# A hybrid HGRN2 and DeltaNet layer: HGRN's first decays made earlier, early tiles in DRAM, state steps in the DeltaNet's buffers

## The chip, the core and the metric

The kernel runs on one core of a Trainium2 chip. The metric is the device time of one execution in microseconds. The engines are PE (TensorE, the matrix engine), ACT (ScalarE), DVE (VectorE), POOL (GpSimd) and SP (SyncE, which here issues loads). Each has its own queue of instructions; DMAs are issued from the queues of SP and POOL.

## The reference

One decoder layer for 512 positions of width 1024. Two token mixers read the same normalised input and are merged by gates; a SwiGLU feed-forward follows.

```python
proj = jnp.einsum('btd,de->bte', rms_norm(x, pre_mix_w), w_in)
# HGRN2: f = lb + (1-lb) sigmoid(f_logit), k = 1 - f,
# S_t = diag(f_t) S_{t-1} + k_t i_t^T, o_t = S_t^T q_t; in chunks:
bc = jnp.cumsum(log_f)                                  # within a chunk
decay = jnp.exp(where(causal, b_c[i] - b_c[j], -inf))   # per channel d
attn = jnp.einsum('bhid,bhjd,bhijd->bhij', q_c, k_c, decay)
o = attn @ v_c + (q_c * jnp.exp(b_c)) @ S
S = S * jnp.exp(b_last) + (k_c * jnp.exp(b_last - b_c)).T @ v_c
# gated DeltaNet: S_t = alpha_t (I - beta_t k_t k_t^T) S_{t-1} + beta_t k_t v_t^T
# chunked with T = (I + A)^-1, A strictly lower triangular
merged = sigmoid(m_a) * (o_a @ w_o_hg) + sigmoid(m_b) * (o_b @ w_o_dn)
h = x + rms_norm(merged @ w_out, post_mix_w)
return h + rms_norm((silu(gate) * up) @ w_down, post_ffn_w)
```

HGRN's decay is per channel, so `attn` is not one matmul of q and k.

## The kernel before

All products are made in three matmuls of split numbers: each float32 operand is a high part (a cast on ACT, L108 for weights, L120 for data) and a low part (a subtraction on DVE, L109 or L146), and `mm3` adds high by high, high by low and low by high. `dense_in` takes one weight tile of 128 output features (512 KB, loaded by SP into `raw`), splits it into `whi` and `wlo`, and runs 24 matmuls of 128x512 into one of three banks `mm`; an evacuation function then empties the bank. The names hg_q, hg_f, hg_g, dn_q, dn_v, dn_g, m_a and m_b are four (or eight) such weight tiles each; hg_q[1] is the second tile of hg_q.

The sequence of work that bears on the change: hg_f, dn_q, dn_v and dn_g are projected. `l2` normalises the DeltaNet's key and query; its column sums (`colsum`, L376 and L377) are matmuls with ones, one for the high and one for the low half of the squares, placed behind named dense matmuls. `dn_sub` runs a forward substitution on POOL in 62 instructions, writes its result to the DRAM scratch `scr` (L460, L462) and reads it back (L483, L486). `hg_prep` makes k (`hk`) and the cumulative log decay b (`hf`) from the f logits, in four chunks of 128 positions. hg_q and half of hg_g are then projected and kept in six `hct` buffers, while `dn_inv` (L479 to L523) completes the DeltaNet's inverse with small matmuls placed between the dense ones; `dn_prep` and `dn_step` run the DeltaNet over its chunks. After it the slots of the DeltaNet's key and query take HGRN's q (`hq`) and gate (`ghg`), into which POOL copies the six buffers (L792, L794). The gate m_b0 is written to DRAM as `early_b` (L786) and read back at L809.

`hg_attn(c)` builds the attention of one chunk from pieces of halving block size, lev = 64, 32, 16, 8, 4, 2. For each lev it makes a tile E of decays, from half of b minus a reference column (two subtractions on POOL, L146), an exponential on ACT (L660), and multiplications by q and by k on DVE (L146); four matmuls of E by itself follow (L667 for lev 64 and 32, L673 below), and their result is copied under a mask into the attention AT (L669, L674). `hg_step(c)` carries the state. Chunk c+1's attention is interleaved with chunk c's step and with dense matmuls of m_b0, hg_g, the DeltaNet's output projection `y_proj` and m_b1.

Buffers are pools: `dct` of nine and `hct` of seven tiles of 128x512, banks `dps` (three) and `hps` (two). Which instruction stands where in a queue is decided by the scheduler of the tile framework at build time, by priorities and estimated times; on the chip each queue runs in that order. POOL's queue holds its subtractions and the DMAs that it issues.

## Time and profile before

| | us |
|---|---|
| median of 3 runs (lowest to highest) | 858.56 (858.18 to 858.79) |
| profiled execution | 856.74 |
| its span in the trace | 855.0 |
| PE busy | 821.0 (96%) |
| DVE busy | 585.6 (68%) |
| ACT busy | 485.4 (57%) |
| POOL busy | 136.9 (16%) |

The profiled execution's own time is 1.74 us above its span, and 1.82 us below the median of the runs. The mean granted clock of TensorE in it was 0.988. Busy shares are averages over the whole program; what ends a wait at one place is read from the timeline there. In the rows further down a time is the microseconds from the span's start. A bracket at the end of a row is the idle time of that engine just before, with what ended it. The duration of an ACT or DVE row includes about 0.1 us in which the next one is already under way, so spacings of starts are a little smaller.

### The profile page before, as it was taken

Reading aid. Unit: us, or ns where it says so; the run is one execution under the profiler, and the core shown is the slowest. Engines: PE = TensorE matmul, PEld = TensorE weight load, DVE = VectorE, ACT = ScalarE, POOL = GpSimd, SP = SyncE. Lnnn points to the kernel's source line nnn. Section 1 sums busy time; section 2 is a strip of 40 time slices with the busy share of each in tenths; the row PEclk is TensorE's granted clock in tenths of the full one; section 3 lists DMA queues with packets and bytes.
Section 4 is the critical chain, followed back from the end, with each engine's and each line's share of the span. In section 5 each row is a group of like instructions: output and inputs, shape, how many; then the busy total and the mean of one; then the engine's idle time right before and its main releaser. Section 6 shows DMA issues by size and latency. Waiting matters only on the chain.

```text
span 855.0 us, 12316 instructions
## 1 busy us (share of the span) xinstructions
PE 821.0 (96%) x4677; PEld 689.3 (81%) x4677; DVE 585.6 (68%) x903; ACT 485.4 (57%) x884; POOL 136.9 (16%) x187
## 2 busy tenths in 40 slices
PE   9998999999997999899999999999999998999995
PEld 8886887767876877788888898999999997876774
DVE  4794998625557788862664797787787787557545
ACT  6658798945376466585443365545455456445443
POOL 1420178300034245430010300000000000000000
PEclk9998999999999999999999999999999999999999
DMA  8425532712126112253211313322413404556552
GB/s 294 153 94 177 140 108 74 179 51 74 38 86 209 51 49 87 87 173 97 86 53 49 123 50 100 116 82 99 145 54 99 148 24 141 181 172 206 186 175 99
DMA packets 34907, 98.53 MB, mean 115 GB/s; under 512 B 4192, under 2 KB 4608, under 8 KB 34720
## 3 DMA queue, kind: packets, MB, share of 16 engines
q1 hardware_dynamic: 32112, 88.65, 31.5%
q0 software_dynamic: 2736, 9.09, 4.0%
q8 instruction: 37, 0.61, 0.3%
q14 instruction: 22, 0.18, 0.1%
HBM read 91.95 MB, written 5.78 MB: 114 GB/s over the span
## 4 chain that ended last, share of the span: by engine, by line
PE 66%; DVE 12%; DMA 11%; ACT 6%; issue 3%; POOL 0%; SPq 0%; DVEq 0%; ACTq 0%; POOLq 0%
PE mm L116 20%; PE mm L117 11%; DMA raw<-in_w_down_dram 8%; DVE wlo L109 3%; PE hps L116 3%; ACT whi L108 3%; DVE hct L146 3%; PE hps L1041 2%; PE hps L1040 2%; PE hps L1042 2%; PE hps L117 2%; DVE s L149 2%; PE hps L673 2%; DVE s L146 1%; PE mm L898 1%
## 5 line engine op out<-in xcount | busy, mean ns | idle before, releaser
L116 PE MATMUL mm<-s,whi 128*128 128x512 f32 (+1 forms) x992 | 310.5, 392 | 0.0
L109 DVE TENSOR_TENSOR wlo<-raw,whi 128x1024 fp32r<-128x1024 f32 x108 | 135.5, 1254 | 116.2 <-ACT whi L108 111.7
L116 PEld LDWEIGHTS mm<-s,whi 128*128 128x128 f32 x992 | 184.3, 190 | 36.5 <-issue 0.2
L117 PE MATMUL mm<-s,wlo 128*128 128x512 f32 (+1 forms) x496 | 196.9, 397 | 0.2 <-DVE wlo L109 0.2
L108 ACT CAST whi<-raw 128x1024 fp32r<-128x1024 f32 x108 | 113.1, 1047 | 80.2 <-DMA raw<-in_w_down_dram 37.9
L117 PEld LDWEIGHTS mm<-s,wlo 128*128 128x128 f32 x496 | 94.0, 189 | 20.2 <-DVE wlo L109 0.7
L146 POOL TENSOR_TENSOR s<-s,dct 128x512 f32<-128x512 f32 (+1 forms) x9 | 12.7, 1437 | 391.0 <-DVE s L149 362.1
L120 ACT CAST whi<-raw 128x512 fp32r<-128x512 f32 (+1 forms) x64 | 38.9, 617 | 28.2 <-PE mm L1041 10.1
L120 ACT CAST whi<-s 128x512 fp32r<-128x512 f32 x42 | 25.9, 617 | 49.4 <-PE mm L116 23.6
L1040 PE MATMUL hps<-s,whi 128*128 128x256 f32 x168 | 47.2, 281 | 0.4 <-DVE hct L146 0.4
L1041 PE MATMUL hps<-s,whi 128*128 128x256 f32 x168 | 47.2, 281 | 0.1
L1042 PE MATMUL hps<-s,wlo 128*128 128x256 f32 x168 | 46.9, 279 | 0.0
L146 DVE TENSOR_TENSOR wlo<-raw,whi 128x512 fp32r<-128x512 f32 (+1 forms) x64 | 43.5, 688 | 2.4 <-ACT whi L120 1.6
L146 POOL TENSOR_TENSOR hct<-s 128x256 f32<-128x256 f32 (+1 forms) x55 | 38.2, 724 | 25.8 <-DVE hct L146 8.6
L116 PE MATMUL hps<-s,whi 128*128 128x512 f32 (+1 forms) x144 | 40.8, 368 | 0.0
L146 DVE TENSOR_TENSOR hct<-hct,s 128x256 f32<-128x256 f32 (+1 forms) x63 | 35.0, 601 | 4.6 <-ACT hct L624 2.0
L146 POOL TENSOR_TENSOR s<-s 128x126 f32<-128x126 f32 (+22 forms) x62 | 34.8, 561 | 10.5 <-DMA s<-scr 5.7
L1040 PEld LDWEIGHTS hps<-s,whi 128*128 128x128 f32 x168 | 31.5, 188 | 0.9 <-DVE hct L146 0.6
L1041 PEld LDWEIGHTS hps<-s,whi 128*128 128x128 f32 x168 | 31.7, 188 | 0.6 <-DVE s L146 0.3
L1042 PEld LDWEIGHTS hps<-s,wlo 128*128 128x128 f32 x168 | 31.7, 189 | 0.0
L1041 PE MATMUL mm<-s,whi 128*128 128x256 f32 x112 | 31.5, 281 | 0.0
L1040 PE MATMUL mm<-s,whi 128*128 128x256 f32 x112 | 31.4, 281 | 0.0
(325 smaller groups left out, 1850.0 us busy)
## 6 DMA issues: line engine op xcount, KB each, us to landing
raw<-in_w_in_a_dram SPq DMA_DIRECT2D x44, 512.0 KB, 3.4
raw<-in_w_down_dram SPq DMA_DIRECT2D x44, 512.0 KB, 3.4
s<-in_w_gu_dram SPq DMA_DIRECT2D x56, 256.0 KB, 4.1
raw<-in_w_gu_dram SPq DMA_DIRECT2D x16, 512.0 KB, 3.6
raw<-in_w_o_dram SPq DMA_DIRECT2D x8, 512.0 KB, 3.5
dct<-in_w_out_dram SPq DMA_DIRECT2D x16, 256.0 KB, 4.2
raw<-in_w_iab_dram SPq DMA_DIRECT2D x8, 260.0 KB, 5.9
s<-in_xT_dram SPq DMA_DIRECT2D x8, 256.0 KB, 6.0
```

The costliest lines, as they stand in the source:

```text
L108: nc.scalar.copy(hi[:, :n], raw[:, :n])
L109: nc.vector.tensor_tensor(out=lo[:, :n], in0=raw[:, :n], in1=hi[:, :n].bitcast(F32), op=ALU.subtract)
L116: return [mm(ps, lh, rh, start=start, stop=False), mm(ps, lh, rl, start=False, stop=False), mm(ps, ll, rh, start=False, stop=stop)]
L117: mm(ps, ll, rh, start=False, stop=stop)]
L120: self.nc.scalar.copy(hi, src)
L146: (eng or self.nc.vector).tensor_tensor(out=out, in0=a, in1=b, op=op)
L149: self.nc.vector.scalar_tensor_tensor(out=out, in0=a, scalar=s, in1=b, op0=op0, op1=op1)
L673: T.matmul(ps[:, h, :], E[:, h, :], E[:, h, :], start=True, stop=True)
L898: T.matmul(ps, mh, wl, start=False, stop=False)
L1040: mm(ps, wh[:, k, :], ah[k], start=start and k == 0, stop=False, skip_group_check=True)
L1041: mm(ps, wh[:, k, :], al[k], start=False, stop=False, skip_group_check=True)
L1042: mm(ps, wl[:, k, :], ah[k], start=False, stop=k == 3, skip_group_check=True)
```

## The change

The two subtractions, the exponential and the multiplication by k of a decay tile move into a function `hg_decay`. For chunk 0 and lev 64, 32, 16, 8 and 4 it is called right behind the call of `dn_inv`, and the five tiles stay in `hct` until HGRN's first chunk uses them; the multiplication by q remains in `hg_attn`. The early tiles of hg_q, hg_g and m_b0 pass through one buffer `out` and are written to DRAM; q and the first half of the gate are read back by five DMAs instead of six POOL copies. HGRN's column sums, its lev 1 tile, its state steps and its head norm use `dct` buffers, and the state steps and the head norm use `dps` banks. The query's l2 column sums move from dn_v to dn_g, and `gates_late` is placed behind the key's norm. For hg_g, `gge` is changed like `qe` below.

```diff
+    def spill(self):
+        return self.tp.tile([P, 512], F32, tag="out", name=self.name("out"), bufs=1)
...
     def l2(self, y, qscale, after):
...
-            if qscale:
-                A.activation(t, t, AF.Exp, scale=-0.5, bias=self.lnqs)
-            else:
+            e = A.activation(t, t, AF.Exp, scale=-0.5, bias=self.lnqs) if qscale else \
                 A.activation(t, t, AF.Exp, scale=-0.5)
-            self.tt(y[:, h, :], y[:, h, :], t, ALU.mult)
+            m = nc.vector.tensor_tensor(out=y[:, h, :], in0=y[:, h, :], in1=t, op=ALU.mult)
+        return e, m
...
-    def hg_attn(self, c, out):
+    def hg_decay(self, c, lev):
+        v = lambda x: x.rearrange("p h (n two t) -> p (h n) two t", two=2, t=lev)
+        n = NH * P // (2 * lev)
+        E = self.hct()
+        Ev, bv, kv = v(E), v(self.hf[:, c]), v(self.hk[:, c])
+        ref = bv[:, :, 0, lev - 1:lev].to_broadcast([P, n, lev])
+        self.tt(Ev[:, :, 1, :], bv[:, :, 1, :], ref, ALU.subtract, self.nc.gpsimd)
+        self.tt(Ev[:, :, 0, :], ref, bv[:, :, 0, :], ALU.subtract, self.nc.gpsimd)
+        self.nc.scalar.activation(E, E, AF.Exp)
+        self.tt(Ev[:, :, 0, :], Ev[:, :, 0, :], kv[:, :, 0, :], ALU.mult)
+        return E
+
+    def hg_attn(self, c, out, decays={}):
...
-        pr = self.hct()
+        pr = self.dct()
...
-        ps = self.colsum(pr.rearrange("p h t -> p (h t)"), self.hct, self.hps)
+        ps = self.colsum(pr.rearrange("p h t -> p (h t)"), self.dct, self.hps)
...
-            E = self.hct()
-            Ev, bv, qv, kv = v(E), v(b), v(q), v(k)
-            ref = bv[:, :, 0, lev - 1:lev].to_broadcast([P, n, lev])
-            self.tt(Ev[:, :, 1, :], bv[:, :, 1, :], ref, ALU.subtract, nc.gpsimd)
-            self.tt(Ev[:, :, 0, :], ref, bv[:, :, 0, :], ALU.subtract, nc.gpsimd)
-            A.activation(E, E, AF.Exp)
+            E = decays[lev] if lev in decays else self.hg_decay(c, lev)
+            Ev, qv = v(E), v(q)
             self.tt(Ev[:, :, 1, :], Ev[:, :, 1, :], qv[:, :, 1, :], ALU.mult)
-            self.tt(Ev[:, :, 0, :], Ev[:, :, 0, :], kv[:, :, 0, :], ALU.mult)
...
     def hg_step(self, c, AT):
...
-        o = self.hps()
+        o = self.dps()
...
-            kd = self.hct()
+            kd = self.dct()
...
-            ps = self.hps()
+            ps = self.dps()
...
-            kt = self.hct()
+            kt = self.dct()
...
-        return self.head_norm(c, o, self.ghg, self.ohg, self.hct, self.hps)
+        return self.head_norm(c, o, self.ghg, self.ohg, self.dct, self.dps)
...
     def mixers(self):
...
-        self.l2(self.kT, False, [self.log["hg_f"][i] for i in (30, 34, 38, 42)])
+        norm = self.l2(self.kT, False, [self.log["hg_f"][i] for i in (30, 34, 38, 42)])
...
-        self.gates_late()
+        with self.tc.issue_after(norm[0].ins), self.tc.issue_after(norm[1].ins):
+            self.gates_late()
...
-        self.l2(self.qT, True, [self.log["dn_v"][i] for i in (38, 50, 62, 74)])
...
+        self.l2(self.qT, True, [self.log["dn_g"][i] for i in (6, 18, 30, 42)])
-        early, eg = {}, {}
+        early_q, early_g, early_b = (self.dp.tile([n, P, S], F32, name=f"early_{t}") for n, t in ((4, "q"), (2, "g"), (4, "b")))
         def qe(i, ps):
-            early[i] = self.hct((P, 512))
-            A.copy(early[i], ps)
+            t = self.spill()
+            A.copy(t, ps)
+            nc.gpsimd.dma_start(out=early_q[i], in_=t)
...
         self.dn_inv((self.log["hg_q"] + self.log["hg_g"])[43::3])
+        early_e = {lev: self.hg_decay(0, lev) for lev in HG_LEVELS[:5]}
...
         def gate_out(ft, ps):
-            t = self.hct((P, 512))
+            t = self.spill()
...
-        for i in range(4):
-            nc.gpsimd.tensor_copy(self.hq[:, :, i, :], early[i].rearrange("p (c t) -> p c t", c=NC_))
-        for i in range(2):
-            nc.gpsimd.tensor_copy(self.ghg[:, i, :], eg[i])
+        for c in range(NC_):
+            nc.gpsimd.dma_start(out=self.hq[:, c], in_=early_q[:, :, c * P:c * P + P].rearrange("f p t -> p f t"))
+        nc.gpsimd.dma_start(out=self.ghg[:, :2], in_=early_g.rearrange("f p t -> p f t"))
...
-        run(self.hg_attn(0, at))
+        run(self.hg_attn(0, at, early_e))
```

Line numbers of the changed kernel are three or four higher up to `hg_prep` (L108 is L112 there, L146 is L150), and up to twelve higher behind it (L667 is L677, L786 is L798).

**POOL, from the end of the DeltaNet's forward substitution.** `scr` is its scratch, `early_b` the m_b0 gate. Before:

```order
L460 DMA scr_649<-s_119_787 64x32x16 x2
L462 DMA scr_650<-s_119_787 64x16x32 x2
L483 DMA s_253_1793<-scr_649 32x16x32 x2
L486 DMA s_118_786<-scr_650 128x8x128 x2
L786 DMA early_b<-hct_2271 128x512
L786 DMA early_b<-hct_2307 128x512
```

The changed kernel, where `hct_1979` to `hct_1999` are the five decay tiles of chunk 0 and `s_92` is b:

```order
L463 DMA scr_649<-s_119_787 64x32x16 x2
L465 DMA scr_650<-s_119_787 64x16x32 x2
L486 DMA s_253_1802<-scr_649 32x16x32 x2
L489 DMA s_118_786<-scr_650 128x8x128 x2
L150 TENSOR_TENSOR hct_1979<-s_92_672 128x4x64 x2
L150 TENSOR_TENSOR hct_1984<-s_92_672 128x8x32 x2
L150 TENSOR_TENSOR hct_1989<-s_92_672 128x16x16 x2
L150 TENSOR_TENSOR hct_1994<-s_92_672 128x32x8 x2
L150 TENSOR_TENSOR hct_1999<-s_92_672 128x64x4 x2
L769 DMA early_q<-out_1623 128x512
```

The ten subtractions stand between the reads of the scratch and the first write of an early tile.

**ACT, around the weight cast for hg_q[1].** `s_210` is k and `s_92` b, `s_193` is the gate of dn_g, whose third tile is `mm_1400`, and `whi_1623` the weights of hg_q[1]. Before:

```order
L108 CAST whi_1623<-raw_1622 128x1024
L141 ACTIVATE s_193_1323<-mm_1400 128x512
L618 ACTIVATE s_210_1464<-s_210_1464,sm_638 128x128
L142 ACTIVATE s_193_1323<-s_193_1323,one 128x512
L620 ACTIVATE hct_1549<-s_92_672,sm_639 128x128
L143 ACTIVATE s_193_1323<-s_193_1323 128x512
L618 ACTIVATE s_210_1464<-s_210_1464,sm_638 128x128
```

The changed kernel, with dn_g's gate as `s_177`, its third tile as `mm_1352` and the weights of hg_q[1] as `whi_1627`:

```order
L623 ACTIVATE hct_1552<-s_92_672,sm_639 128x128
L642 ACTIVATE hct_1979<-hct_1979 128x512
L112 CAST whi_1627<-raw_1626 128x1024
L145 ACTIVATE s_177_1275<-mm_1352 128x512
L626 ACTIVATE hct_1552<-hct_1552 128x512
L146 ACTIVATE s_177_1275<-s_177_1275,one 128x512
L627 ACTIVATE hct_1552<-hct_1552,one 128x512
L147 ACTIVATE s_177_1275<-s_177_1275 128x512
L642 ACTIVATE hct_1984<-hct_1984 128x512
L642 ACTIVATE hct_1989<-hct_1989 128x512
L642 ACTIVATE hct_1994<-hct_1994 128x512
L642 ACTIVATE hct_1999<-hct_1999 128x512
```

The exponential of the first decay tile stands ahead of the cast and of the evacuation of dn_g's third tile, and the other four stand behind that evacuation.

**DVE, at the third step of the DeltaNet.** `s_299` is the DeltaNet's output, `wlo_2530` the low weights of the second late tile of hg_g, and `dct_2216` the low half of a column sum. Before:

```order
L146 TENSOR_TENSOR dct_2173<-dct_2115,dct_2172 128x512
L146 TENSOR_TENSOR dct_2117<-dct_2117,dct_2115 128x512
L146 TENSOR_TENSOR s_299_2047<-dct_2117,s_298_2046 128x4x128
L109 TENSOR_TENSOR wlo_2530<-raw_2528,whi_2529 128x1024
L146 TENSOR_TENSOR dct_2213<-dps_2202,s_193_1323 128x512
L146 TENSOR_TENSOR dct_2216<-dct_2168,dct_2215 128x512
L146 TENSOR_TENSOR dct_2228<-dct_2211,dct_2227 128x512
```

The changed kernel, with the output as `s_304`, the low weights as `wlo_2537`, the low half as `dct_2250`, and HGRN's q as `s_371`:

```order
L150 TENSOR_TENSOR dct_2207<-dct_2149,dct_2206 128x512
L150 TENSOR_TENSOR dct_2151<-dct_2151,dct_2149 128x512
L150 TENSOR_TENSOR hct_1979<-hct_1979,s_371_2417 128x4x64
L150 TENSOR_TENSOR hct_1984<-hct_1984,s_371_2417 128x8x32
L150 TENSOR_TENSOR s_304_2081<-dct_2151,s_303_2080 128x4x128
L150 TENSOR_TENSOR hct_1989<-hct_1989,s_371_2417 128x16x16
L150 TENSOR_TENSOR hct_1994<-hct_1994,s_371_2417 128x32x8
L150 TENSOR_TENSOR hct_1999<-hct_1999,s_371_2417 128x64x4
L113 TENSOR_TENSOR wlo_2537<-raw_2535,whi_2536 128x1024
L150 TENSOR_TENSOR dct_2247<-dps_2236,s_177_1275 128x512
L150 TENSOR_TENSOR dct_2250<-dct_2202,dct_2249 128x512
```

The five multiplications of the decay tiles by q stand ahead of the weight split and of the DeltaNet's column sum.

**PE, at the first L667 of HGRN** (L677 in the changed kernel). `mm_2534` is the second late tile of hg_g and `mm_3040` the first of the DeltaNet's output projection. Before:

```order
L116 MATMUL mm_2534<-s_64_568,whi_2529 128x512
L116 MATMUL mm_2534<-s_66_570,whi_2529 128x512
L117 MATMUL mm_2534<-s_64_568,wlo_2530 128x512
L667 MATMUL hps_2422<-hct_2416 64x64 x4
L667 MATMUL hps_2434<-hct_2428 32x32 x4
L116 MATMUL mm_3040<-s_298_2046,whi_3035 128x512
L116 MATMUL mm_3040<-s_299_2047,whi_3035 128x512
L117 MATMUL mm_3040<-s_298_2046,wlo_3036 128x512
```

The changed kernel, where `mm_2506` is the first late tile of hg_g and `hps_2444` the column sum of lev 1:

```order
L380 MATMUL hps_2444<-dct_2440,onesr 128x256
L677 MATMUL hps_2449<-hct_1979 64x64 x3
L381 MATMUL hps_2444<-dct_2441,onesr 128x256
L677 MATMUL hps_2449<-hct_1979 64x64
L120 MATMUL mm_2506<-s_64_568,whi_2501 128x512
L120 MATMUL mm_2506<-s_66_570,whi_2501 128x512
L121 MATMUL mm_2506<-s_64_568,wlo_2502 128x512
L677 MATMUL hps_2456<-hct_1984 32x32 x4
L683 MATMUL hps_2468<-hct_1989 128x128 x4
```

The first decay matmuls come 28 instructions earlier, within the tile ahead.

## Rows read from the trace of the kernel before

**Rows 1.** The page: busy time, share of the span and instructions of each engine.

```profile
PE 821.0 (96%) x4677; PEld 689.3 (81%) x4677; DVE 585.6 (68%) x903; ACT 485.4 (57%) x884; POOL 136.9 (16%) x187
```

**Rows 2.** Stretches: length, busy of PE, PEld, DVE, ACT, POOL, clock, DMA share, GB/s.

```profile
258.60:370.30 111.70, 101.23 (x594) 81.09 (x593) 90.96 (x144) 65.93 (x118) 48.81 (x67) 0.97 0.28 90
275.40:281.60 6.20, 6.13 (x37) 5.24 (x37) 4.56 (x6) 1.66 (x4) 1.91 (x2) 0.51 0.22 67
300.00:320.00 20.00, 18.17 (x107) 14.03 (x105) 17.33 (x30) 12.63 (x22) 9.87 (x13) 1.00 0.13 46
320.00:340.00 20.00, 19.53 (x123) 15.71 (x119) 18.04 (x31) 13.02 (x24) 9.04 (x12) 1.00 0.25 80
340.00:360.00 20.00, 16.65 (x108) 13.66 (x109) 15.55 (x24) 13.28 (x24) 11.43 (x16) 1.00 0.27 83
```

**Rows 3.** Timeline of PE: start, duration, instruction, and idle time before it.

```profile
141.36 0.50 PE L377 MATMUL dps<-dct,onesr 128*128 128x512 f32 x1 [1.51 <-DVE dct L146]
...
177.70 0.43 PE L479 MATMUL dps<-s,dct 32*32 32x32 f32 x8
...
256.15 0.50 PE L377 MATMUL dps<-dct,onesr 128*128 128x512 f32 x1 [1.05 <-DVE dct L146]
...
269.90 0.63 PE L116 MATMUL mm<-s,whi 128*128 128x512 f32 x2
270.37 0.40 PE L117 MATMUL mm<-s,wlo 128*128 128x512 f32 x1
275.47 1.69 PE L667 MATMUL hps<-hct 128*64 128x64 f32 x16 [4.71 <-DVE hct L146]
...
344.10 0.65 PE L667 MATMUL hps<-hct 128*64 128x64 f32 x8 [1.98 <-DVE hct L146]
```

**Rows 4.** Timeline of POOL, where the change takes away or adds work.

```profile
160.19 1.80 POOL L486 DMA_DIRECT2D s<-scr  x2 [1.38 <-DMA scr<-s]
...
245.91 2.29 POOL L792 COPY s<-hct 128x512 f32<-128x512 f32 x4 [5.28 <-PE dps L556]
...
267.52 0.78 POOL L809 DMA_DIRECT2D s<-early_b  x1 [3.75 <-issue]
268.32 7.48 POOL L146 TENSOR_TENSOR hct<-s 128x256 f32<-128x256 f32 x12
```

**Rows 5.** Timeline of ACT, around dn_g and the first tiles of hg_q.

```profile
140.13 0.59 ACT L141 ACTIVATE s<-mm 128x512 f32<-128x512 f32 x1
141.89 0.69 ACT L387 ACTIVATE dct<-dps,eps 128x512 f32<-128x512 f32 x1 [1.17 <-PE dps L377]
142.48 0.71 ACT L142 ACTIVATE s<-s,one 128x512 f32<-128x512 f32 x1
...
163.44 1.05 ACT L108 CAST whi<-raw 128x1024 fp32r<-128x1024 f32 x1 [0.16 <-PE mm L116]
164.39 0.58 ACT L757 COPY hct<-mm 128x512 f32<-128x512 f32 x1
...
166.10 1.14 ACT L143 ACTIVATE dct<-dct 128x512 f32<-128x512 f32 x2
```

**Rows 6.** DMA issues from 60 to 380 us: size of one, median us to landing.

```profile
early_b<-hct POOLq DMA_DIRECT2D x4, 256.0 KB, 4.1
...
s<-scr POOLq DMA_DIRECT2D x2, 256.0 KB, 6.5
```

**Rows 7.** Timeline of DVE, from the third DeltaNet step to HGRN's first decays.

```profile
253.93 2.77 DVE L146 TENSOR_TENSOR dct<-dct,dct 128x512 fp32r<-128x512 f32 x2 [0.34 <-ACT dct L120]
...
264.25 0.89 DVE L146 TENSOR_TENSOR hct<-hct,s 128x256 f32<-128x256 f32 x2 [0.54 <-ACT hct L645]
...
270.22 5.86 DVE L146 TENSOR_TENSOR hct<-hct,s 128x256 f32<-128x256 f32 x3 [1.17 <-ACT hct L660]
```

**Rows 8.** DVE's groups by shape, 258.6 to 370.3 us: busy, mean ns, idle before.

```profile
L146 DVE TENSOR_TENSOR hct<-hct,s 128x256 f32<-128x256 f32 x56 | 30.0, 584 | 2.4 <-ACT hct L660 1.7 <-ACT hct L645 0.5
L109 DVE TENSOR_TENSOR wlo<-raw,whi 128x1024 fp32r<-128x1024 f32 x11 | 14.9, 1354 | 0.9 <-ACT whi L108 0.8
```

More of the change, by code (lines that the diff above doesn't have):

```diff
@@ L642, in hg_attn @@
         bv, qv, kv, av = v(b), v(q), v(k), v(AT)
-        E = self.hct((P, NH, 64))
+        E = self.dct((P, NH, 64))
         self.tt(E, bv[:, :, :, 1], bv[:, :, :, 0], ALU.subtract, nc.gpsimd)
@@ L647, in hg_attn @@
         self.tt(E, E, kv[:, :, :, 0], ALU.mult)
-        ps = self.colsum(E.rearrange("p h n -> p (h n)"), self.hct, self.hps, 256)
+        ps = self.colsum(E.rearrange("p h n -> p (h n)"), self.dct, self.hps, 256)
         V.copy_predicated(av[:, :, :, 1], self.hgm[1].rearrange("p (n two) -> p n two", two=2)[:, :, 1].bitcast(U32)
@@ L690, in hg_step @@
             self.tt(kd, kd, k, ALU.mult)
-            ps = self.hps()
+            ps = self.dps()
             for h in range(NH):
                 T.transpose(ps[:, h, :], kd[:, h, :], self.ident)
-            kt = self.hct()
+            kt = self.dct()
             A.copy(kt, ps)
-            ps = self.hps()
+            ps = self.dps()
             for h in range(NH):
@@ L748, in mixers @@
         self.dense_in("dn_v", self.conv_evac(self.vT, 8))
-        self.l2(self.qT, True, [self.log["dn_v"][i] for i in (38, 50, 62, 74)])
         self.gdn = self.slot(5, [P, NH, S])
         self.dense_in("dn_g", self.gate_evac(self.gdn, self.dnw))
-        early, eg = {}, {}
+        self.l2(self.qT, True, [self.log["dn_g"][i] for i in (6, 18, 30, 42)])
+        early_q, early_g, early_b = (self.dp.tile([n, P, S], F32, name=f"early_{t}") for n, t in ((4, "q"), (2, "g"), (4, "b")))
         def qe(i, ps):
-            early[i] = self.hct((P, 512))
-            A.copy(early[i], ps)
+            t = self.spill()
+            A.copy(t, ps)
+            nc.gpsimd.dma_start(out=early_q[i], in_=t)
         def gge(i, ps):
-            eg[i] = self.hct((P, 512))
-            self.sigmoid(eg[i], ps)
-            self.stt(eg[i], ps, self.hnw, eg[i], ALU.mult, ALU.mult)
+            t = self.spill()
+            self.sigmoid(t, ps)
+            self.stt(t, ps, self.hnw, t, ALU.mult, ALU.mult)
+            nc.gpsimd.dma_start(out=early_g[i], in_=t)
         self.hg_prep()
@@ L779, in mixers @@
         run(prev)
-        early_b = self.dp.tile([4, P, S], F32, name="early_b")
         def gate_out(ft, ps):
-            t = self.hct((P, 512))
+            t = self.spill()
             self.sigmoid(t, ps)
```

1 line of the change is left out of this document (removed).

## The prediction

> **What bounds the kernel now.** Read the page's busy times first: the matrix engine (PE) is busy 821.0 of 855.0 us [rows 1], so only about 34 us of idle, and the stretches in which its clock is low, can be won. The table by stage [rows 2] shows where: from 258.6 to 370.3 us, where HGRN's chunks run between dense matmuls, PE is busy 101.23 of 111.70 us. The timeline of PE [rows 3] names the largest wait there, 4.71 us before the first L667, which waited for VectorE (DVE); behind it the granted clock was 0.51 of full, the lower level of 1.2 GHz, for 6.2 us [rows 2]. Two more waits lie elsewhere: 1.51 us at 141.36 (a column sum of the query's l2 norm) and 1.05 us at 256.15.
>
> Where the 4.71 us come from is read on GpSimd (POOL) [rows 4]: the read L809, queued behind the last write of early_b, was issued at 267.52, and only then ran the twelve subtractions of HGRN's first decays, 7.48 us or 0.62 us each; ScalarE's (ACT) exponentials and DVE's multiplications follow, and then L667.
>
> **First decays: the new wait.** Ten subtractions, five exponentials and five multiplications by k are moved from there to the end of the gate preparation. The count of each stays; what matters is what they are queued behind. On POOL they stand behind the DeltaNet's forward substitution and behind L483 and L486, whose issue waited for earlier transfers; the last L486 ended at 160.19 + 1.80 = 161.99 us [rows 4]. Nothing of that is removed, so the first pair of subtractions ends at 162.0 + 2 x 0.62 = 163.2, and the others follow at 1.25 us each.
>
> On ACT the first exponential stands directly ahead of the cast of the weights of hg_q[1] and ahead of the evacuation of dn_g[2]. ACT gets there at about 148 us: the cast for hg_q[0] becomes free when dn_g[1] is through, by my count of matmuls at 143.1, and then come 0.95 us and twelve short operations (4.0 us). So ACT stands still from 148 to 163.2, though its work is ready. That an instruction of ACT waits for the one ahead of it, whatever its own inputs, is seen at 140.13 [rows 5]: L141 ended at 140.72, L142 needed only that, but stood behind L387, which waited until 141.89 for PE, and started at 142.48. A rule of the Trainium skill says the same (Perfetto Trace Analysis, section Tensor Engine Instruction (MATMUL, LD_WEIGHTS)): ACT, DVE and GpSimd are strict first in, first out. By that rule the wait holds up all that is behind it and the time is the one forecast here; were it otherwise the block would not exist and the third rival below would hold. The trace agrees, with those 1.76 us.
>
> What PE loses: hg_q[0] ended at 163.4 in the profile, where the cast at 163.44 waited for it [rows 5]. Without the 1.51 us and two column sums that move (0.5), it ends at 161.4. hg_q[1] then needs its weights and the bank of dn_g[2]. From 163.2: exponential 0.52, cast 0.95, then L141, L623, L142, L624, L143 at 0.5 to 0.6 (2.75) and DVE's evacuation with its start (0.9), 168.4 in all [rows 5]. **PE waits 7.0 us.** Ten matmuls on, it needs the fourth column sum of the query's norm. Its cast is eighteen ACT instructions behind 167.5: the four other exponentials, the evacuation of dn_g[3], seven operations of the norm, two weight casts and the rest, two of 0.95 and sixteen of about 0.55, 10.7 us, so 178.2. PE, which has done ten matmuls (2.35 us, at 0.235 [rows 3]), stands **another 7.4 us**. After that 38 matmuls (8.9 us), two column sums (0.5) and 27 small inverse matmuls (at about 0.09, 2.4) bring it to the place that the profile has at 177.70 [rows 3]: 178.2 + 11.9 = 190.1, **12.4 us later**, the gain of 1.51 us already in it.
>
> The clock can add to that. Behind the 4.71 us wait it was low for 6.2 us, which costs 3.0; behind the 1.98 us wait at 344.10 no such stretch followed [rows 2, 3]. A drop behind the first wait is swallowed by the second; one behind the second adds up to 3.0. So 12.4 to 15.4, and I take 14.0, since both waits are longer than the one that had it. The Trainium skill (TensorE: Matmul & The Clock Gate, section HAM oscillation) holds that gaps of this kind put the array back on the slow clock each time. By it the upper end, 15.4, would be right and the forecast 1.4 us longer; the row of the 4.71 us wait agrees, the one of 1.98 us shows that not every gap does it.
>
> **Tiles kept in DRAM.** Six tiles are written (256 KB) through one buffer, so each evacuation waits for the former write. Such a write landed in 4.1 us [rows 6], evacuations are at least 24 matmuls, 5.6 us, apart: nothing, with 1.5 us as slack. The six POOL copies that filled hq and the gate go; five reads replace them, and cannot start before the key's last use, where the copies started too (245.91) [rows 4]. A read of a chunk of hq is bounded by the early_b write, 4.1 us, and by the 256 KB reads from scratch, 6.5 us [rows 6]: landing at 250.0 to 252.4. On DVE the five multiplications by q stand ahead of a weight split and of the two low halves that PE's L377 need. From the landing, five at 0.45 (a pair took 0.89 at 264.25), another at 0.6, the split 1.2, an evacuation 0.6 and the half 0.7 come to 255.3 to 257.7. The profile had this half done at 253.6, where DVE fell idle ahead of 253.93, and the second at about 256, the latter of two that took 2.77 us together while POOL was at work [rows 7]. At the second L377 (256.15) this is 0 to 3.3 us; I take **1.5**, below the middle, since the copies that slowed DVE there are gone.
>
> **HGRN's stage.** Gone are the 4.71 us wait (no subtraction is in that chain any more) and the 3.0 us of low clock. The other waits of the stage are 111.70 - 101.23 - 4.71 = 5.8 us, so 13.5 in all. But the stage is also packed tighter: between its start and the last column sum PE has 344 instructions and had 440, that is 96 fewer dense matmuls (22.5 us) to cover DVE. PE then needs 101.23 - 3.0 - 22.5 = 75.7 us. DVE needs its 90.96 less ten multiplications of 0.584, four splits of 1.354 [rows 8], and four smaller operations that leave the stage (3.6): 76.1. So DVE becomes the bound. At best 0.4 us of waiting remains, a gain of 13.1. At DVE's share in the densest 20 us [rows 2], 18.04/20 = 0.90, it is 84.4 us, a gain of 4.8; at its share from 300 to 360, 50.92/60 = 0.85, 89.7 us, a loss of 0.5. I take a **gain of 7.5**, between the densest stretch and the best, because chunk 0 finds its decays ready, and because part of DVE's idle time was itself waiting for dense matmuls that are no longer in front.
>
> The DeltaNet's banks and buffers for the state steps, the later gate loads and the later loads of w_out I cost at nothing. The m_b1 and m_a matmuls, 5.6 us for each weight tile, hide them; a load landing behind its use would cost up to its 4.1 us once.
>
> **Sum.** +14.0 + 1.5 - 7.5 = +8.0 us. On the profiled execution's own 856.74 that is 864.7; this execution lies 1.8 below the median of the runs, 858.56, so the runs should give **866.5**.
>
> **Rivals.** First, no change: the loss at its least and HGRN's gain at its most, 12.4 + 0 - 13.1 = -0.7, with the middle of this case at +1, 859.5. For it speaks that the sum hangs on DVE's share, which no row of before fixes; against it, that DVE was never above 0.90 for 20 us.
>
> Second, HGRN's stage turns wholly into waiting for DVE: 15.4 + 3.3 + 0.5 = +19 at most, about +14 in the middle, 872.5. It decides from DVE's share falling to 0.85; the multiplications next to POOL's subtractions at 270.22, 5.86 us for three groups [rows 7], speak for it.
>
> Third, faster: the block does not form, because the exponentials find their inputs when ACT gets there. PE would have nothing to wait for if the first subtractions ended by 163.2 - 7.0 = 156.2, that is if POOL were through 7 us earlier, or if the waiting exponential let others pass. Then -2.0 + 1.5 - 7.5 = -8.0, 850.5. Against it stand the 161.99 of L486 and the place of the instructions, which is fixed.
>
> **How the numbers follow.** About 0.2%, 1.7 us, is what a measurement of this kernel can tell from no change. Forecast (860.3 to 871) 0.62, second rival 0.12, first rival 0.13, third 0.13. The range runs from 858, the lower end of the sum, to 874; below it lie the third rival and a part of the first, above it a small part of the second. Faster 0.14, same 0.12, slower 0.74.
>
> **What would show it.** Right: on ACT an idle time of about 15 us ended by POOL before the first moved exponential; on PE two waits near 161 and 171 us of about 7 us each, ended by DVE and ACT; no wait of over 1 us before the first L667; DVE over 0.88 busy through HGRN. Wrong: ACT's wait under 8 us, or PE with no wait over 3 us between 155 and 180, makes the loss fall away; waits of over 8 us in HGRN's stage would put the gain in question.

## The result, and the profile after

| | before | after |
|---|---|---|
| median (lowest to highest) | 858.44 us (852.2 to 859.17, 9 runs) | 862.71 us (859.2 to 864.52, 9 runs) |
| profiled execution, its span | 856.74, 855.0 | 861.81, 859.9 |
| mean granted clock in it | 0.988 | 0.986 |

After to before is 1.0061, 95% interval 1.0044 to 1.0079: slower by 4.3 us between the medians. The forecast was slower by 8.0 (866.5 us); the time lies inside its range of 860.3 to 871, near the lower end.

The busy times of PE, DVE and ACT hardly moved; POOL's rose by 10.3 us. The page's first line of after, beside [rows 1]:

```profile
PE 820.4 (95%) x4677; PEld 689.9 (80%) x4677; DVE 585.6 (68%) x903; ACT 483.7 (56%) x884; POOL 147.2 (17%) x192
```

What moved is where PE waits. Nearly all line numbers of after are higher by four or more: the dense matmuls L116 and L117 are L120 and L121, the column sums L376 and L377 are L380 and L381, L667 is L677, DVE's and POOL's L146 is L150, and the decays' exponential is L642. POOL's timeline of after (start, duration, instruction, idle time before it), at the place of the first of [rows 4]:

```profile
155.31 1.80 POOL L489 DMA_DIRECT2D s<-scr  x2
157.12 7.13 POOL L150 TENSOR_TENSOR hct<-s 128x256 f32<-128x256 f32 x10
```

ACT's timeline of after, where the first moved exponential stands:

```profile
145.96 0.39 ACT L623 ACTIVATE hct<-s,sm 128x128 f32<-128x128 f32 x1
158.35 0.63 ACT L642 ACTIVATE hct<-hct 128x512 f32<-128x512 f32 x1 [12.01 <-POOL hct L150]
158.89 1.03 ACT L112 CAST whi<-raw 128x1024 fp32r<-128x1024 f32 x1
...
172.86 0.63 ACT L124 CAST dct<-dct 128x512 fp32r<-128x512 f32 x1
```

And PE's timeline of after, for the block and for the first L677, which had waited 4.71 us as L667 [rows 3]:

```profile
165.52 1.22 PE L120 MATMUL mm<-s,whi 128*128 128x512 f32 x2 [7.76 <-DVE s L153]
...
173.54 0.54 PE L380 MATMUL dps<-dct,onesr 128*128 128x512 f32 x1 [3.39 <-ACT dct L124]
...
276.46 0.56 PE L677 MATMUL hps<-hct 128*64 128x64 f32 x6
```

The chain reads from top to bottom. POOL can begin the first decays only when its last scratch read is issued, at 157.1; ACT, whose own work is ready, stands for 12.01 us in front of the exponential that needs them; behind it stand the weight cast (158.89) and the evacuation that PE needs, so PE stops twice, 11.15 us together. The first L677 waits no more. By stretches (start and end, length, busy of PE, PEld, DVE, ACT and POOL, granted clock, DMA share, GB/s), after:

```profile
140.00:160.00 20.00, 17.75 (x77) 14.07 (x75) 7.89 (x14) 7.55 (x17) 15.62 (x25) 1.00 0.52 121
160.00:180.00 20.00, 11.09 (x36) 7.83 (x36) 14.88 (x21) 17.23 (x30) 4.84 (x7) 0.66 0.32 105
270.20:352.90 82.70, 76.47 (x496) 61.87 (x495) 74.03 (x120) 47.75 (x90) 42.50 (x52) 1.00 0.26 78
```

ACT, idle for most of 140 to 160, is busy for 17.23 of the next 20 us, in which PE runs 36 matmuls at a mean clock of 0.66. The third line is HGRN's stage, from its start to its last column sum, beside the first of [rows 2]: 82.7 us with 496 matmuls, for 111.7 us with 594, since 97 dense matmuls now come behind it.

**Where each microsecond went.** The program has 120 dense weight tiles of 24 matmuls, the same in all kernels. The table lists when tile 8, 20, 24 and 41 start, in three stretches, as the difference from the first profile of before (there they start at 83.27, 157.94, 189.68 and 373.09 us). Tiles 20 to 24 hold the block; 24 to 41 hold the rest of the DeltaNet and HGRN's stage. One profiled execution stands behind each row; the ratio is of the medians, with its interval, against the kernel before, measured together with it. The ratio of late_exp leaves out two slow executions of its twelve (868.34 and 872.3 us, at a mean clock of 0.967 and 0.962), which the medians in the text include. The kernels are those of the next section.

| kernel | to tile 8 | 8 to 20 | 20 to 24 | 24 to 41 | ratio (interval) |
|---|---|---|---|---|---|
| before_again | -1.2 | 0.0 | 0.0 | +0.6 | 0.9978 (0.9961 to 0.9996) |
| gates_alone | -4.0 | -0.3 | 0.0 | +1.2 | 0.9975 (0.9959 to 0.9991) |
| gates_l2 | -3.0 | -2.3 | -0.4 | +1.3 | 0.9927 (0.9902 to 0.9951) |
| dram_undone | -3.1 | -2.3 | -0.4 | -1.1 | 0.9907 (0.9886 to 0.9929) |
| no_early | -4.5 | -2.3 | -0.4 | -1.4 | 0.9908 (0.9881 to 0.9934) |
| **after** | -3.6 | -2.2 | **+14.3** | -3.7 | 1.0061 (1.0044 to 1.0079) |
| gates_undone | -3.3 | -2.3 | +13.8 | -5.3 | 1.0062 (1.004 to 1.0083) |
| own_bufs | -2.8 | -2.3 | +14.5 | -4.6 | 1.0024 (0.9999 to 1.005) |
| late_exp | -3.2 | -2.2 | +11.2 | -4.1 | 0.9972 (0.9951 to 0.9994) |
| late_spill | -3.1 | -2.2 | -0.3 | -3.6 | 0.9927 (0.9894 to 0.9959) |
| sub_dve | -0.1 | -2.3 | +0.1 | -5.4 | 0.9888 (0.9862 to 0.9914) |
| sub_q | +0.3 | -2.3 | +0.2 | -5.2 | 0.9896 (0.9872 to 0.9919) |
| sub_own | -2.6 | -2.3 | +0.2 | -6.0 | 0.9857 (0.983 to 0.9883) |

### The profile page after: what moved, and what is told of

It is laid out like the page before. It is cut to its first block, busy times and chain, and to the rows that moved or that the text cites. A ratio compares the mean times of both kernels' runs of the same rounds, so it can differ in the third digit from the quotient of the medians.

```text
span 859.9 us, 12321 instructions
## 1 busy us (share of the span) xinstructions
PE 820.4 (95%) x4677; PEld 689.9 (80%) x4677; DVE 585.6 (68%) x903; ACT 483.7 (56%) x884; POOL 147.2 (17%) x192
## 4 chain that ended last, share of the span: by engine, by line
PE 55%; DMA 11%; DVE 8%; POOL 6%; ACT 5%; issue 3%; SPq 0%; DVEq 0%; ACTq 0%; POOLq 0%
PE mm L120 15%; DMA raw<-in_w_down_dram 8%; PE mm L121 8%; POOL s L150 4%; PE hps L120 3%; ACT whi L112 3%; DVE wlo L113 3%; PE hps L1052 2%; PE hps L1051 2%; PE hps L1053 2%; PE hps L121 2%; PE dps L1052 1%; PE dps L1051 1%; PE dps L1053 1%; PE mm L1052 1%
## 5 line engine op out<-in xcount | busy, mean ns | idle before, releaser
L120 PE MATMUL mm<-s,whi 128*128 128x512 f32 (+1 forms) x992 | 310.5, 393 | 7.8 <-DVE s L153 7.8
L113 DVE TENSOR_TENSOR wlo<-raw,whi 128x1024 fp32r<-128x1024 f32 x108 | 139.0, 1287 | 127.5 <-ACT whi L112 124.0
L120 PEld LDWEIGHTS mm<-s,whi 128*128 128x128 f32 x992 | 184.7, 190 | 45.6 <-DVE s L153 8.2
L121 PE MATMUL mm<-s,wlo 128*128 128x512 f32 (+1 forms) x496 | 196.9, 397 | 0.0
L112 ACT CAST whi<-raw 128x1024 fp32r<-128x1024 f32 x108 | 113.0, 1046 | 93.3 <-DMA raw<-in_w_down_dram 41.9
L121 PEld LDWEIGHTS mm<-s,wlo 128*128 128x128 f32 x496 | 94.5, 191 | 20.3 <-DVE wlo L113 0.2
L150 POOL TENSOR_TENSOR s<-s,dct 128x512 f32<-128x512 f32 (+1 forms) x9 | 12.7, 1437 | 392.0 <-DVE s L153 362.4
L150 DVE TENSOR_TENSOR wlo<-raw,whi 128x512 fp32r<-128x512 f32 (+1 forms) x64 | 43.5, 688 | 2.7 <-ACT whi L124 1.8
L120 PE MATMUL hps<-s,whi 128*128 128x512 f32 (+1 forms) x144 | 40.8, 368 | 0.0
L150 POOL TENSOR_TENSOR hct<-s 128x256 f32<-128x256 f32 x48 | 36.9, 796 | 10.9 <-PE dps L694 5.0
L150 DVE TENSOR_TENSOR hct<-hct,s 128x256 f32<-128x256 f32 (+1 forms) x52 | 27.2, 567 | 14.4 <-ACT hct L642 12.0
L150 POOL TENSOR_TENSOR s<-s 128x126 f32<-128x126 f32 (+22 forms) x62 | 34.2, 551 | 11.1 <-DMA s<-scr 6.4
```

What stands on the lines that cost most here:

```text
L112: nc.scalar.copy(hi[:, :n], raw[:, :n])
L113: nc.vector.tensor_tensor(out=lo[:, :n], in0=raw[:, :n], in1=hi[:, :n].bitcast(F32), op=ALU.subtract)
L120: return [mm(ps, lh, rh, start=start, stop=False), mm(ps, lh, rl, start=False, stop=False), mm(ps, ll, rh, start=False, stop=stop)]
L121: mm(ps, ll, rh, start=False, stop=stop)]
L150: (eng or self.nc.vector).tensor_tensor(out=out, in0=a, in1=b, op=op)
```

## The experiments

The theory to be tested is the prediction's: the time after is a loss in one block, made by one queue waiting for another, and a smaller gain in HGRN's stage. The rivals: the block is plain overload of ACT or DVE, wherever the decays stand; and the gain is not the early decays' but that of another part of the change.

**no_early** and **sub_dve: the block.** The first takes the early decays away; the second leaves them early and moves their ten subtractions from POOL to DVE.

```diff
-        early_e = {lev: self.hg_decay(0, lev) for lev in HG_LEVELS[:5]}
...
-        run(self.hg_attn(0, at, early_e))
+        run(self.hg_attn(0, at))
```

> The changed kernel without the first decays ahead: all decay tiles of chunk 0 are made in HGRN's stage again, and the tiles in DRAM, the buffers, the gate loads and the norm's place stay. The block theory takes 14 us off and puts back the wait of the kernel before ahead of the first decay matmul (4.7 us there) with its stretch at the lower clock (3 us): 855 to 858 us. If the early decays gave HGRN's stage nothing (its gain coming from the buffers and banks), 848 to 851 us.

```diff
-        early_e = {lev: self.hg_decay(0, lev) for lev in HG_LEVELS[:5]}
+        early_e = {lev: self.hg_decay(0, lev, nc.vector) for lev in HG_LEVELS[:5]}
```

> The changed kernel, with the ten subtractions of the first decays on DVE instead of POOL; the exponentials stay where the projection of hg_q runs. Block theory: they find their inputs, since DVE is not queued behind the DeltaNet's forward substitution; ACT has no idle time of over 3 us ended by a decay, PE's waits of 7.8 and 3.4 us go, and 4.5 to 6 us of added DVE work lies in DVE's idle time there: 849 to 853 us. Overload theory: the work of ACT is the same as in the changed kernel, so PE waits near 160 to 175 us stay, 858 us or more.

Measured: no_early 847.57 us (845.18 to 850.02), sub_dve 846.18 us (844.1 to 848.58). Both lose the whole block (20 to 24: -0.4 and +0.1), and PE is busy through it, in sub_dve's stretches (columns as above):

```profile
140.00:160.00 20.00, 20.00 (x88) 16.19 (x87) 19.09 (x38) 19.51 (x37) 13.88 (x24) 1.00 0.46 112
160.00:180.00 20.00, 19.51 (x159) 14.07 (x157) 9.65 (x14) 17.53 (x37) 3.46 (x5) 1.00 0.52 172
```

So it is not overload: DVE takes ten more instructions and ACT the same exponentials. sub_dve is not one change alone, since the scheduler also placed the first exponential anew, behind the weight cast for hg_q[1] and the evacuation of dn_g[2]. ACT's timeline of sub_dve:

```profile
150.33 1.03 ACT L112 CAST whi<-raw 128x1024 fp32r<-128x1024 f32 x1
151.27 0.59 ACT L145 ACTIVATE s<-mm 128x512 f32<-128x512 f32 x1
...
152.98 0.61 ACT L642 ACTIVATE hct<-hct 128x512 f32<-128x512 f32 x1
```

late_spill, below, shows the same with the subtractions still on POOL. So it is the order of two queues that made the loss: subtractions behind POOL's scratch reads, and ahead of PE's needs on ACT an exponential that waits for them.

no_early came out at the other reading in its expectation, a little below its 848: without early decays the first L677 waits 0.77 us, not 4.71. POOL's timeline of no_early shows why:

```profile
246.51 0.58 POOL L797 DMA_DIRECT2D early_b<-out  x1 [2.20 <-ACT out L147]
...
250.00 9.88 POOL L150 TENSOR_TENSOR hct<-s 128x256 f32<-128x256 f32 x11
...
262.72 0.80 POOL L819 DMA_DIRECT2D s<-early_b  x1 [0.43 <-issue]
```

In before the twelve subtractions of HGRN's first decays came behind the read of early_b [rows 4]; here eleven begin 12.7 us ahead of it.

**late_exp** and **late_spill: two queues in a row.** In the first all five decays are queued behind the eighth evacuation of the inverse. That moves the exponentials in ACT's queue and the multiplications by k in DVE's; on POOL the subtractions still come right behind the scratch reads. The second also issues the copies of the early q tiles to DRAM from ACT.

```diff
+                    self.inva = A.mul(U[c][L, :, H], ps[L, :, :32], -1.0)
...
-        early_e = {lev: self.hg_decay(0, lev) for lev in HG_LEVELS[:5]}
+        with self.tc.issue_after(self.inva.ins):
+            early_e = {lev: self.hg_decay(0, lev) for lev in HG_LEVELS[:5]}
```

> The changed kernel, with the ten subtractions, five exponentials and five multiplications of the first decays queued on ACT behind the eighth small product of the DeltaNet's inverse (L501 of before) instead of ahead of the weight cast for hg_q[1]. Block theory (ACT stands behind an exponential that waits for POOL): ACT's idle time of 12.0 us near 146 to 158 us goes, PE's waits of 7.8 and 3.4 us between 157 and 174 us go, and so do the two stretches at the lower clock behind them; dense tile 22 starts some 6 us before the kernel before instead of 9.3 us behind it. Time 848 to 850 us, 13 to 14 us under the changed kernel. Overload theory (ACT has too much to do there, since five exponentials and the query's norm were moved in): at most half of it, 856 us or more, with PE still waiting over 3 us for ACT or DVE between 155 and 185 us.

Measured: 853.89 us, above the 848 to 850 of the theory and short of its rival. ACT no longer waits for the subtractions, but the loss in the block is still 11.2 us. POOL's timeline of late_exp:

```profile
158.35 8.44 POOL L150 TENSOR_TENSOR hct<-s 128x256 f32<-128x256 f32 x10
166.75 0.59 POOL L769 DMA_DIRECT2D early_q<-out  x1
```

ACT's of late_exp:

```profile
169.18 0.59 ACT L768 COPY out<-mm 128x512 f32<-128x512 f32 x1 [4.44 <-DMA early_q<-out]
```

PE's of late_exp:

```profile
172.71 0.46 PE L482 MATMUL dps<-s,s 32*32 32x32 f32 x8 [2.80 <-ACT dct L497]
```

The copy of the first q tile to DRAM is an instruction of POOL behind the same subtractions. That was its place in after too, but there ACT emptied the tile only at 171.45 us, and here it does at 158.37. The one buffer `out` stays full, the next evacuation waits for it on ACT for 4.44 us, and PE waits 2.80 us for what is behind that. Then the clock takes over. Stretch of late_exp (columns as above):

```profile
173.10:193.50 20.40, 20.40 (x126) 12.69 (x124) 3.04 (x4) 7.79 (x20) 0.54 (x1) 0.50 0.18 63
```

PE is busy for all of the 20.4 us, at the lower level, 1.2 GHz. In the same microseconds late_spill ran 178 matmuls:

```profile
173.10:193.50 20.40, 20.40 (x178) 13.35 (x175) 7.80 (x13) 13.69 (x31) 0.00 (x0) 1.00 0.24 78
```

```diff
-            nc.gpsimd.dma_start(out=early_q[i], in_=t)
+            A.dma_start(out=early_q[i], in_=t)
```

> The kernel with the exponentials queued late (853.9 us), and the copies of HGRN's early q tiles to DRAM issued by ScalarE in place of GpSimd. Theory: what kept that kernel from the full gain is the GpSimd queue: the copy of the second q tile stood behind the ten subtractions (158.35 to 166.75 us), so the one spill buffer came free at 169.18 us, ScalarE waited 4.44 us, TensorE 2.80 us, and the clock halved from 173.0 to 193.5 us. Then 843 to 848 us here, no stretch at half clock between 160 and 200 us. Rival: ScalarE is overloaded there anyway: 851 us or more.

Measured: 850.33 us (847.07 to 857.51), the profiled execution 848.43. The block is gone (-0.3) and no stretch between 160 and 200 us is at half clock, as the theory said; the median is above its 848, and the runs of this kernel spread over 10 us, which stays unexplained.

**own_bufs** and **sub_own: the state steps.** HGRN's state steps and their norm go back to HGRN's buffers and banks, in after and in sub_dve.

```diff
-        o = self.dps()
+        o = self.hps()
...
-            kd = self.dct()
+            kd = self.hct()
...
-        return self.head_norm(c, o, self.ghg, self.ohg, self.dct, self.dps)
+        return self.head_norm(c, o, self.ghg, self.ohg, self.hct, self.hps)
```

> The changed kernel with HGRN's state steps back in HGRN's own buffers and banks (hct and hps in place of dct and dps), the first decays still made early. Theory A: the kernel without early decays kept a short HGRN stage, so the gain of that stage comes from the seven buffers and the banks that the state steps no longer take: here the stage (from dense tile 24 to 41) loses 3 to 6 us against the changed kernel, 865.5 to 869 us. Theory B: it comes from the early decays, which stay: 861.5 to 864 us.

> The kernel with the first decays' subtractions on VectorE (0.9888 of before, 846.2 us), and HGRN's state steps back in HGRN's own buffers and banks. Theory: the state steps in the DeltaNet's buffers gain nothing (the changed kernel was 859.1 with them undone, 862.7 with them), so 843 to 846.5 us, 0.985 to 0.989 of before. Rival: with the block gone, the borrowed buffers are what lets HGRN's stage run close, and undoing them costs 3 to 6 us, 849 to 852 us.

Measured: 859.09 us (853.3 to 865.84; after 862.71) and 845.71 us (842.62 to 846.14; sub_dve 846.18). The stretch from tile 24 to 41 is 0.9 and 0.6 us shorter with this part undone, not 3 to 6 longer. The state steps in the DeltaNet's buffers gain nothing; whether they cost something stays open, since the intervals of after and own_bufs meet. sub_own has the lowest time of all, but its interval overlaps that of sub_dve.

**dram_undone: tiles in DRAM.** From no_early, the six early tiles stay in `hct` and POOL copies them, as before.

```diff
-            t = self.spill()
-            A.copy(t, ps)
-            nc.gpsimd.dma_start(out=early_q[i], in_=t)
+            early[i] = self.hct((P, 512))
+            A.copy(early[i], ps)
...
-            nc.gpsimd.dma_start(out=self.hq[:, c], in_=early_q[:, :, c * P:c * P + P].rearrange("f p t -> p f t"))
+            nc.gpsimd.tensor_copy(self.hq[:, :, i, :], early[i].rearrange("p (c t) -> p c t", c=NC_))
```

> The changed kernel without early decays (0.9908 of before, 847.6 us), and with HGRN's six early tiles kept in SBUF and copied by GpSimd as before. Theory: the re-read from DRAM costs what the prediction took for it, 1.5 us, so this is 845 to 847 us. Rival: keeping six of the seven hct buffers through the DeltaNet's steps is what the spill frees, and without early decays nobody needs them there: 847 to 849 us, no change. Second rival: GpSimd's six copies cost more than five reads, 849.5 us or more.

Measured: ratio 0.9907 beside 0.9908, no change: the first rival. Without early decays the copies to DRAM are worth and cost nothing. This kernel's POOL runs its eleven subtractions early too, so that is not the spill's doing either:

```profile
251.47 9.89 POOL L150 TENSOR_TENSOR hct<-s 128x256 f32<-128x256 f32 x11
...
264.19 0.80 POOL L820 DMA_DIRECT2D s<-early_b  x1 [0.44 <-issue]
```

In gates_l2, which has every buffer as before, they come behind the read again:

```profile
262.64 0.78 POOL L809 DMA_DIRECT2D s<-early_b  x1 [4.48 <-issue]
263.44 7.48 POOL L146 TENSOR_TENSOR hct<-s 128x256 f32<-128x256 f32 x12
```

Between these two lie HGRN's column sums, the early_b tiles and the state steps, which no longer take `hct` (or `hps`). That the freed buffers let the subtractions come early is argued from these orders; which of the three frees them was not run by itself.

**sub_q: the re-read of q.** In sub_dve the multiplications by q are queued behind the low half of the DeltaNet's last column sum.

```diff
-            self.tt(Ev[:, :, 1, :], Ev[:, :, 1, :], qv[:, :, 1, :], ALU.mult)
+            with self.tc.issue_after(self.qlo.ins) if lev in decays else nullcontext():
+                self.tt(Ev[:, :, 1, :], Ev[:, :, 1, :], qv[:, :, 1, :], ALU.mult)
```

> The kernel with the first decays' subtractions on VectorE (846.2 us), and its multiplications by q queued on VectorE behind the first chunk's last column sum, so that no DeltaNet work stands behind the re-read of q from DRAM (there 2.84 us at 249 us). Theory: 1.5 to 3 us of that reach the end, 843 to 845 us. Rival: TensorE has other work then, or HGRN's stage is bound by VectorE (busy 19.3 us of each 20 from 280 to 320 us), and the time stays within 845 to 847.5 us.

Measured: 848.17 us, ratio 0.9896 beside 0.9888; the theory's 843 to 845 missed. DVE's wait for the re-read, 2.84 us in sub_dve, is not in sub_q's timeline, and PE's wait at the column sum fell from 2.70 to 1.13 us. It bought nothing, as the rival had it: beside sub_dve, the 1.9 us gained from tile 24 to 30 were lost again from 30 to 41 (2.1 us).

**gates_alone, gates_undone, before_again, gates_l2: what happened before the block.** Tile 8 starts 3.6 us earlier in after, and no step of the prediction had that. The move of `gates_late` is the only edit written there; the four runs do it alone, undo it, repeat before unchanged, and add the moved norm of the query. The expectations call it the gate loads, but no DMA moves: what goes behind the key's norm is work of DVE and ACT that needs the loaded gates, first of all a copy (L341, L345 in after).

```diff
-        self.gates_late()
+        with self.tc.issue_after(norm[0].ins), self.tc.issue_after(norm[1].ins):
+            self.gates_late()
```

> The kernel before, with the late gate loads queued behind the key's norm, and nothing else of the change. Theory: DVE no longer stands for 4.7 us behind a copy that waits for the read of gd (69.65 us in the trace of before), the wait of 1.26 us of PE at 74.23 goes, and with it the stretch of 6.8 us at the lower clock: 4.2 us less, 854.2 us. Rival: that low clock comes and goes from execution to execution whatever the order there: 857 to 858.5 us.

> The changed kernel with the DeltaNet's gate loads put back where they were before. Theory (the step that the prediction costed at nothing): alone, the move shortened the span by the 4.0 us between 70 and 80 us, where VectorE had waited 4.71 us for the loads; with that undone here, the time is 862.7 + 3 to 5 = 865.5 to 868 us, and TensorE falls to half clock before 80 us again. Rival: the wait there only changes places with the block at 158 us or the clock, 861.5 to 864 us.

> The kernel before, profiled once more, nothing changed. Theory: the late landing of the gate loads between 65 and 80 us (VectorE waits 4.71 us, then 6.8 us at half clock) belongs to one execution of this kernel, not to its order of loads: here VectorE's wait for them differs by over 1 us, and dense tile 8 starts 1.5 to 4.5 us earlier than the 83.27 us of the first profile. Rival: it belongs to the order of the loads: the wait is within 0.5 us of 4.71 us and the tile starts at 83.3 us within 0.7 us. The time is that of the kernel before by either, 852 to 860 us.

Measured: gates_alone 853.59, gates_undone 862.69, before_again 855.33 us. gates_undone, with `gates_late` in its old place, starts tile 8 early by 3.3 us too, and its time is after's: the rival. DVE's wait for the read of `gd`, the DRAM scratch of the DeltaNet's gates, had been 4.71 us in the first profile of before. Timeline of DVE in before_again, and below it in gates_undone:

```profile
66.64 0.18 DVE L341 COPY sm<-s 128x16 f32<-128x16 f32 x1 [1.83 <-DMA s<-gd]
```

```profile
66.79 0.18 DVE L345 COPY sm<-s 128x16 f32<-128x16 f32 x1 [1.99 <-DMA s<-gd]
```

So that length was one execution's. But before_again's tile 8 gained 1.2 us, not the 1.5 that was expected. Its ratio to itself, 0.9978 with an interval that leaves out 1, also says how far such an interval can be trusted: the 0.9975 of gates_alone can't be told from it. The move is worth somewhere from nothing to 2 us, and these runs do not settle it.

```diff
-        self.l2(self.qT, True, [self.log["dn_v"][i] for i in (38, 50, 62, 74)])
...
+        self.l2(self.qT, True, [self.log["dn_g"][i] for i in (6, 18, 30, 42)])
```

> The kernel before with the later gate loads and the query's norm moved behind the dn_g tiles, nothing else. Theory: the 1.51 us wait of TensorE at 141 us and two column sums leave that place, 2.0 us under the later gate loads alone (0.9975 of before), so 0.9945 to 0.996 of before, some 852 us. Rival: the norm's ScalarE work in its new place holds up the DeltaNet's gates: 0.9975 or more.

Measured: 851.44 us, ratio 0.9927: faster than the theory's 0.9945 to 0.996. The stretch from tile 8 to 20, the one that this edit touches, is 2.0 us shorter than in gates_alone (-2.3 beside -0.3), as priced; the rest of the difference in the medians is in no stretch of the profiles.

## Why the prediction was right, and where its numbers came from

**First decays: right, in mechanism and nearly in size.** The step forecast that ACT stands in front of the first exponential until POOL is through with the scratch reads, and that PE then waits twice. ACT waited from 146.3, not 148, to 158.35, 12.0 for 15.2 us, because POOL, like all that lies ahead, was 5 us early by then. From there to the end of PE's second wait the run took 15.2 us, where the working has 15.0 (163.2 to 178.2). The two waits themselves came out at 7.76 and 3.39 us where 7.0 and 7.4 stood, for two reasons that both moved time within the block. The working let PE go on 0.9 us after ACT was through with dn_g[2]; it took 2.9 (162.6 to 165.52), since DVE had a multiplication by k and a weight split to do first, both slow beside POOL's subtractions. DVE's timeline of after:

```profile
159.02 3.10 DVE L150 TENSOR_TENSOR hct<-hct,s 128x256 f32<-128x256 f32 x1 [11.99 <-ACT hct L642]
162.04 1.74 DVE L113 TENSOR_TENSOR wlo<-raw,whi 128x1024 fp32r<-128x1024 f32 x1
...
166.67 1.40 DVE L150 TENSOR_TENSOR hct<-hct,s 128x256 f32<-128x256 f32 x4
```

And the clock fell during the first wait already: the ten matmuls between the waits ran at half clock and took 4.6 us for the 2.35 of the working. The second wait took up both, as the prediction had it for the clock. By its end the block cost 14.3 us, the norm's move in front of it gained 2.2, together 12.1 for 14.0, just under the 12.4 to 15.4 of the working. Undone in two ways, the whole time fell by 13.1 and 14.8 us by the ratios (0.9908 and 0.9888 for 1.0061, of some 856.5 us). The Trainium skill (TensorE: Matmul & The Clock Gate, section HAM oscillation) says that a gap in PE's work puts it back on the slow clock; for the waits of 7.76, 3.39 and, in late_exp, 2.80 us the trace agrees, at 0.50 from 160.2, 173.9 and 173.0. That level then held until 170.5, 177.3 and 193.5.

The third rival, that the block doesn't form, was worked out at 850.5 us; sub_dve is that case by another road, at 846.2.

**Tiles kept in DRAM: +1.5 forecast.** DVE does wait for the re-read, and PE behind it. Timelines of DVE and of PE in after, the second at the column sum that waited 1.05 us before [rows 3]:

```profile
259.07 0.76 DVE L150 TENSOR_TENSOR hct<-hct,s 128x256 f32<-128x256 f32 x2 [2.14 <-DMA s<-early_q]
```

```profile
264.60 0.51 PE L381 MATMUL dps<-dct,onesr 128*128 128x512 f32 x1 [2.30 <-DVE dct L150]
```

PE's wait grew by 1.25 us, near the 1.5 of the working. But the clock then was at 0.50 from 266.0 to 269.5, 1.7 us more, and the step had no clock in it: from tile 24 to 30 after lost 3.2 us, and gates_undone, with the same wait and the clock at 1.00, lost 1.8. Yet neither taking the copies away (dram_undone, where nothing early waits for them) nor taking the wait away (sub_q) moved the time. The step missed a price of another kind too: each copy out is an instruction in POOL's queue, which costs nothing where POOL is free and, in late_exp, held ACT for 4.44 us.

**HGRN's stage: size right, cause half wrong.** The working had the packed stage at 111.7 - 22.5 - 7.5 = 81.7 us, with PE busy for 75.7 and DVE for 76.1. It took 82.7, with 76.5 and 74.0: a gain of 6.5, DVE at a share of 0.90. The second rival, which began at a share of 0.85, did not come. What was wrong is whose gain it is. The step held that the 4.71 us wait goes because the decays are made early; no_early and dram_undone are rid of all but 0.8 us of it without them; the buffers are the likely cause, which was argued above and not shown. What the early decays add is 2.3 us from tile 24 to 41 in after and 4.0 in sub_dve (-3.7 and -5.4 beside -1.4), part of it the clock, which is low for 6.8 us of that stretch in no_early and for 3.4 in these two. In the medians sub_dve and no_early cannot be told apart. So 14 us were paid for at most 4.

**Ahead of the block: not forecast, and not settled.** The working put nothing there; in the profiles 3.6 us lie there. The profiled execution of before, on which the sum was made, had half clock from 73.3 to 80.1 us, behind a late load; that of after had not. Before profiled again had it for 3.4 us, and own_bufs, gates_l2, dram_undone, sub_dve and sub_q, all with `gates_late` moved, had it as well, for 3.4 or 6.8 us. So part of it belongs to executions and not to kernels. What differs between executions can be read in the traces: POOL reads `gd` back once its write has landed. POOL's row in after, the same in before_again, and an ACT row of before_again:

```profile
62.58 0.58 POOL L339 DMA_DIRECT2D s<-gd  x1 [3.72 <-DMA gd<-sm]
```

```profile
60.51 0.58 POOL L335 DMA_DIRECT2D s<-gd  x1 [2.41 <-DMA gd<-sm]
```

```profile
68.84 1.05 ACT L108 CAST whi<-raw 128x1024 fp32r<-128x1024 f32 x1 [1.60 <-DMA raw<-in_w_in_a_dram]
```

In four profiles POOL waited only 2.3 to 2.5 us for that write (before_again, gates_undone, sub_dve, sub_q). In each of them that weight cast of ACT then stood 1.0 to 1.7 us for its load, and PE 2.9 to 3.8 us at the key's first column sum, with `gates_late` in either place. In the other ten POOL waited 3.7 to 4.1 us and that cast not at all; there PE waited 1.8 us in the nine with `gates_late` moved, and 2.02 and 1.26 us at two column sums in the one with the old place, the first profile of before. So the move shows no gain in the first case, and in the second a gain that rests on a single profile. Ten of the twelve changed kernels reach tile 8 from 2.6 to 4.5 us ahead of the first profile of before, gates_undone among them, and before itself only 1.2. Something in the change may be worth 2 us there; the move of `gates_late` was tried and is not shown to be it.

**The sum.** In the spans 4.9 us were measured for 8.0. The difference of -3.1 is made of -3.6 unforeseen, -1.9 at the block with the norm, +1.7 at the tiles in DRAM, +0.5 at HGRN's stage (tile 30 to 41) and +0.2 behind it. That -1.9 and +1.7 cancel is luck.

## What to carry over

When work is moved to an idle stretch, look at the queue that it enters: here the stretch could take the work (in sub_dve PE is busy for all of 140 to 160 us), and the loss was ten subtractions behind the scratch reads on POOL, with ACT waiting in front of what PE needed. With the same ten instructions on DVE, and the order on ACT that came with it, a kernel 0.6% slower than before became one 1.1% faster. And before a part of a change is credited, run the change without it: the wait that the early decays were to remove was gone without them too.
